# Three of eight convolution blocks as VectorE multiply-adds, shifted copies through DRAM, and second operands in PSUM, in a one-layer hybrid decoder block

## The chip, the cores and the metric

The kernel runs on one core of a Trainium2 chip. The metric is the device time of one launch in microseconds. TensorE is written PE in the rows, VectorE DVE, ScalarE ACT, GpSimd POOL, and SyncE, which issues the DMA transfers, SP. PEld is TensorE's weight load, which runs beside its matmuls.

## The reference, cut to what is computed

One layer, 256 tokens, 2048 channels, all in fp32. A norm is followed by one input projection that feeds two groups of heads; their outputs are joined and pass one output projection; then come a squared-ReLU MLP of 8192 channels and a gated embedding.

```python
h = rms_norm(x, norm_mix_pre)
z = h @ w_in                                   # 2048 -> 3360 (RWKV) + 2048 (conv)
z_rwkv = z[:, :3360] + (shift(z[:, :3360]) - z[:, :3360]) * mu
y_rwkv = rwkv7_time_mix(z_rwkv, ...)           # 16 heads of 64, recurrent over tokens
y_conv = conformer_conv(z[:, 3360:])
mixed = concat(y_rwkv, y_conv) @ w_out
x = x + rms_norm(mixed, norm_mix_post)
f = square(relu(rms_norm(x, norm_mlp_pre) @ w_up)) @ w_down
x = x + rms_norm(f, norm_mlp_post)
x = x + sigmoid(x @ w_ple_gate) * rms_norm(p @ w_ple, norm_ple)

def conformer_conv(z):                         # 1024 channels
    u = z_lin * sigmoid(z_gate)
    c = causal_depthwise_conv(u, dw_w, width=31) + dw_b
    c = (c - mean(c)) * rsqrt(var(c) + eps) * ln_gain + ln_bias   # over the channels
    return silu(c)
```

## The kernel before

Activations lie transposed: 128 channels on the partitions, 256 tokens along a row. Every product with a large weight is made in three parts (high part by high part, high by low, low by high): a 1 MB weight unit `W` comes by DMA, ScalarE casts quarters of it to `wh`, GpSimd (at times VectorE) subtracts to get `wl`, and TensorE runs 16 steps of three matmuls into a PSUM bank `acc` (lines 434 to 436; 439 to 442 where two parts share an instruction). There are two `W` buffers, seven `wh`/`wl` quarters and, in the first half of the layer, two `acc` banks; the tags `wk` and `inv` have two banks each, `seq` and `psy` one.

The order of instructions is fixed when the kernel is built. Each piece of work is a generator that yields operations; a planner (class `Plan`) keeps a clock for each engine with estimated costs (`tt`, `stt`, `ts`, `act`, `copy`, `pe`, `dma_in`), takes the operation that can start first, and among those that can start within 40 ns on that engine the one with the lowest priority number. The instructions then run on each engine, and on SP's DMA queue, in exactly this order and wait for their inputs. The helpers give many operations one line: 246 is any VectorE `tt`, 252 any `stt`, 248 any GpSimd `tt`, 276, 277 and 285 ScalarE, 231 any load.

The first half has 43 input tiles in an order written out by hand (`ORDER`: "p" a pair of heads with its tiles k, r, v; "c" a convolution block with its tiles linear and gate): p0, c0, c1, p1, p2, c2, c3, p3, c4, c5, c6, p4, c7, p5, p6, p7. Then come 32 half tiles of the output projection, first the convolution half, then the RWKV half. A tile's result is evicted by a generator: `zshift` for the pairs' tiles (VectorE multiplies by the norm into `zp`, ScalarE scales it into `zt`, VectorE combines both), `ev_lin` and `ev_gate` for the convolution. Each pair then runs `decay`, `keys`, `chunk_mats`, `values`, `bonus`, `inverse`, `recur` and `group_norm`; `recur` is serial over the pairs.

A convolution block of 128 channels (`taps`, priority 4) puts four shifted copies of `u`, each for 32 channels at a time, into the staging tile `cvst`: 16 matmuls with slices of the identity (line 1044) into `wk`, and two ScalarE copies. Then eight rounds of four matmuls with 32 columns each (line 1056) take four taps a round into an `inv` bank, with weights `cw` that come by DMA. An fp32 matmul stands twice in the rows. When all eight blocks are done, `layer_norm` (priority 1) runs over them on VectorE, GpSimd and ScalarE. The second half of the layer (up, down, gate) isn't touched by the diff.

## Time and profile before

| what | us |
|---|---|
| median of 3 runs (range) | 1400.93 (1400.87 to 1402.88) |
| the profiled execution's own time | 1402.03 |
| its span, first to last instruction | 1400.2 |
| TensorE busy, share of the span | 1351.5, 97% |
| GpSimd busy | 1174.2, 84% |
| ScalarE busy | 799.4, 57% |
| VectorE busy | 736.4, 53% |

The profiled execution is one run with the profiler on; its rows are from the slowest, here the only, core. Busy time is the union of an engine's instructions; matmuls overlap one another, so that a row's mean duration is longer than the distance between two starts. A wait is put down to the engine that released it last.

### The profile page before, as it was taken

The numbers are of one execution on the slowest core, as the hardware profiler recorded it, in microseconds if no ns is written. First come the engines' busy times: TensorE is split into PE (matmuls) and PEld (weight loads), VectorE is DVE, ScalarE is ACT, GpSimd is POOL, SyncE is SP. The second block draws the span as 40 slices with busy tenths as digits, with TensorE's granted clock in tenths as the row PEclk, the third lists the DMA queues.
The fourth block names the chain that finished last, engine by engine and source line by source line (L and its number), as shares of the span: only waits on it lengthen the run. The fifth ranks groups of instructions, "written<-read, shape, count | busy, mean of one in ns | idle before, by whom it ended". The sixth has DMA issues, their size and how long they took to land.

```text
span 1400.2 us, 27458 instructions
## 1 busy us (share of the span) xinstructions
PE 1351.5 (97%) x10476; PEld 1182.8 (84%) x10476; DVE 736.4 (53%) x1305; ACT 799.4 (57%) x1667; POOL 1174.2 (84%) x1002
## 2 busy tenths in 40 slices
PE   8999999999789999999999999999999999999898
PEld 7868878788778998788888888888888888889688
DVE  7256837235886545687003663236632266433694
ACT  6835665556657656855445554455554455555853
POOL 7765756576777769789999999999999999999787
PEclk9999999999899999999999999999999999999999
DMA  7442333433222465345555554555554555555353
GB/s 243 159 140 95 115 130 113 137 110 137 91 99 95 153 248 182 128 160 194 211 182 191 194 185 181 183 189 194 187 181 182 187 194 189 181 181 190 124 198 120
DMA packets 40354, 229.40 MB, mean 164 GB/s; under 512 B 6304, under 2 KB 9632, under 8 KB 14624
## 3 DMA queue, kind: packets, MB, share of 16 engines
q1 hardware_dynamic: 40224, 227.66, 46.0%
q8 instruction: 82, 1.34, 0.4%
q14 instruction: 48, 0.39, 0.1%
HBM read 225.55 MB, written 2.10 MB: 163 GB/s over the span
## 4 chain that ended last, share of the span: by engine, by line
PE 86%; DVE 8%; ACT 2%; issue 1%; DMA 1%; POOL 1%; SPq 0%; DVEq 0%; ACTq 0%; POOLq 0%
PE acc L441 34%; PE acc L442 17%; PE acc L434 8%; PE acc L435 7%; PE acc L436 7%; PE acc L440 3%; PE inv L1056 2%; PE acc L439 1%; PE wk L1044 1%; DVE hl L252 1%; DVE acc L246 1%; DVE acc L252 1%; PE psy L930 1%; PE seq L938 1%; PE wk L749 1%
## 5 line engine op out<-in xcount | busy, mean ns | idle before, releaser
L248 POOL TENSOR_TENSOR wl<-W,wh 128x512 fp32r<-128x512 f32 x548 | 734.4, 1353 | 119.2 <-ACT wh L285 99.3
L285 ACT CAST wh<-W 128x512 fp32r<-128x512 f32 x568 | 346.3, 618 | 220.3 <-PE acc L440 69.0
L441 PE MATMUL acc<-hl,wh 128*128 128x512 f32 x1016 | 369.8, 403 | 11.3 <-DVE hl L252 5.7
L441 PE MATMUL acc<-fhl,wh 128*128 128x512 f32 x806 | 288.2, 395 | 0.0
L442 PE MATMUL acc<-hl,wl 128*128 128x256 f32 x1016 | 286.5, 282 | 0.0
L434 PE MATMUL acc<-hl,wh 128*128 128x256 f32 (+1 forms) x928 | 282.1, 304 | 1.0 <-DVE zp L246 0.9
L436 PE MATMUL acc<-hl,wl 128*128 128x256 f32 (+1 forms) x928 | 265.2, 286 | 6.3 <-POOL wl L248 6.0
L435 PE MATMUL acc<-hl,wh 128*128 128x256 f32 (+1 forms) x928 | 265.7, 286 | 3.2 <-DVE hl L252 2.0
L248 POOL TENSOR_TENSOR wl<-Wb,wh 128x512 fp32r<-128x512 f32 x173 | 237.0, 1380 | 18.4 <-ACT wh L285 11.2
L441 PEld LDWEIGHTS acc<-hl,wh 128*128 128x128 f32 x1016 | 192.1, 189 | 60.2 <-DVE hl L252 8.4
L442 PE MATMUL acc<-fhl,wl 128*128 128x256 f32 x806 | 227.2, 282 | 0.0
L442 PEld LDWEIGHTS acc<-hl,wl 128*128 128x128 f32 x1016 | 193.2, 190 | 3.7
L434 PEld LDWEIGHTS acc<-hl,wh 128*128 128x128 f32 (+1 forms) x928 | 179.2, 193 | 15.6 <-issue 10.1
L246 DVE TENSOR_TENSOR gt<-acc,tb 128x256 f32<-128x256 f32 x124 | 52.4, 423 | 263.7 <-ACT tb L276 263.1
L436 PEld LDWEIGHTS acc<-hl,wl 128*128 128x128 f32 (+1 forms) x928 | 179.1, 193 | 7.3 <-POOL wl L248 6.6
L435 PEld LDWEIGHTS acc<-hl,wh 128*128 128x128 f32 (+1 forms) x928 | 179.5, 193 | 5.4 <-DVE hl L252 3.7
L441 PEld LDWEIGHTS acc<-fhl,wh 128*128 128x128 f32 x806 | 151.5, 188 | 33.4
L285 ACT CAST wh<-Wb 128x512 fp32r<-128x512 f32 x174 | 107.6, 621 | 89.4 <-PE acc L440 35.5
L442 PEld LDWEIGHTS acc<-fhl,wl 128*128 128x128 f32 x806 | 151.3, 188 | 2.7
L246 DVE TENSOR_TENSOR f<-f 128x256 f32<-128x256 f32 x63 | 85.9, 1366 | 1.9
L246 DVE TENSOR_TENSOR fhl<-f,fhl 128x256 fp32r<-128x256 f32 x62 | 58.5, 946 | 26.0 <-ACT fhl L276 26.0
L248 POOL TENSOR_TENSOR wlb<-W,whb 128x512 fp32r<-128x512 f32 x50 | 69.2, 1384 | 1.9 <-ACT whb L285 1.6
(319 smaller groups left out, 2004.2 us busy)
## 6 DMA issues: line engine op xcount, KB each, us to landing
W<-in_w_up_dram SPq DMA_DIRECT2D x43, 1024.0 KB, 4.8
W<-in_w_down_dram SPq DMA_DIRECT2D x42, 1024.0 KB, 4.8
W<-in_w_in_dram SPq DMA_DIRECT2D x38, 1024.0 KB, 4.9
Wb<-in_w_down_dram SPq DMA_DIRECT2D x22, 1024.0 KB, 4.8
Wb<-in_w_up_dram SPq DMA_DIRECT2D x21, 1024.0 KB, 4.8
W<-in_w_out_dram SPq DMA_DIRECT2D x14, 1024.0 KB, 4.8
W<-in_w_gate_dram SPq DMA_DIRECT2D x11, 1024.0 KB, 5.0
Wb<-in_w_gate_dram SPq DMA_DIRECT2D x5, 1024.0 KB, 4.8
```

The source lines that it names most:

```text
L246: alts.append((e, dve, lambda: nc.vector.tensor_tensor(out=out, in0=a, in1=b, op=op), None, pen))
L248: alts.append((e, 220 + 2.27 * n, lambda: nc.gpsimd.tensor_tensor(out=out, in0=a, in1=b, op=op), None, pen))
L252: return Op([("DVE", 210 + 1.042 * n + (0 if self.from_psum(R) or n < 128 else PORT), lambda: self.nc.vector.scalar_tensor_tensor(out=out, ...
L285: alts.append((e, 150 + 0.835 * n, lambda: self.nc.scalar.copy(out, a), None, 0))
L434: return [nc.tensor.matmul(o, h, xk[:, 0, :], start=(i == 0), stop=False), nc.tensor.matmul(o, h, xk[:, 1, :], start=False, stop=False), n ...
L435: nc.tensor.matmul(o, h, xk[:, 1, :], start=False, stop=False),
L436: nc.tensor.matmul(o, l, xk[:, 0, :], start=False, stop=(i == n - 1))]
L439: return [nc.tensor.matmul(a[:cols, T:], l, xk[:, 0, :], start=False, stop=False), nc.tensor.matmul(a[:cols, :], h, both, start=False, sto ...
L440: nc.tensor.matmul(a[:cols, :], h, both, start=False, stop=True)]
L441: return [nc.tensor.matmul(a[:cols, :], h, both, start=(i == 0), stop=False), nc.tensor.matmul(a[:cols, T:], l, xk[:, 0, :], start=False, ...
L442: nc.tensor.matmul(a[:cols, T:], l, xk[:, 0, :], start=False, stop=False)]
L1056: nc.tensor.matmul(ps.t[32 * g:32 * g + 32, :T], cw.t[:, g, m, :], cv.t[:, g, 4 * m:4 * m + T], start=(m == 0), stop=(m == 7)) for g in ra ...
```

## The change

It does four things. The shifted copies of the convolution no longer come from TensorE: `u` is stored to a DRAM tile `ur` and loaded four times, shifted, into `cvst`, all issued from SP's queue (`dma_move`). Blocks 2, 4 and 6 (`DCONV`) take another way altogether: 31 multiply-adds of VectorE with one weight column each (`dw`, new columns of `vecs`), from a padded `u` (`ux`) into an `inv` bank. Several second operands and results that lay in SBUF now lie in the other half of a PSUM bank that is at hand (`zt` and the gate's sigmoid in `acc`, `n4` in its `wk` bank, `ud` in the `inv` bank, the group norm reads `psy` without a copy, its gain product goes to a `wk` bank), so those banks are given back later. The gate product is always VectorE's. The planner's cost for DMA issues changes with it.

```diff
-NV = _o + 3
+VOFF["dw"] = _o + 3
+NV = _o + 3 + 8 * WIDTH
+DCONV = [2, 4, 6]
...
         if eng == "DMA":
-            self.clock["SP"] = st + 60
-            self.dma = max(self.dma, st + 700) + c
-            en = self.dma + 1900
+            self.clock["SP"] = st + (func or 330)
+            if func:
+                en = max(self.dma, st + 700) + c + 3300
+            else:
+                self.dma = max(self.dma, st + 700) + c
+                en = self.dma + 1900
...
+    def dma_move(self, dst, src, nbytes, R, W, rel=()):
+        return Op([("DMA", nbytes / 150.0, lambda: self.nc.sync.dma_start(dst, src), 600, 0)], R, W, rel)
...
+    dr = pa.enter_context(tc.tile_pool(name="dr", bufs=2, space=bass.MemoryType.DRAM))
+    reg(dr, "ur", 2, [P, 3 + T])
...
-    def scaled(acc, o, W, cols=P):
+    def scaled(acc, o, W, cols=P, keep=False):
-        yield pl.tt(["DVE"], o, acc.t[:cols, :T], r.t[:cols], ALU.mult, T, [acc, r], [W], [acc])
+        yield pl.tt(["DVE"], o, acc.t[:cols, :T], r.t[:cols], ALU.mult, T, [acc, r], [W], [] if keep else [acc])
     def zshift(acc, o, W, mu, j=0, cols=P):
-        yield from scaled(acc, zp.t[:cols, 1:], zp, cols)
+        yield from scaled(acc, zp.t[:cols, 1:], zp, cols, True)
-        d = yield Take("zt", 1)
-        yield pl.act(d.t[:cols], zp.t[:cols, 1:], AF.Identity, T, [zp, "omu"], [d], scale=om)
+        d = acc.t[:cols, T:]
+        yield pl.act(d, zp.t[:cols, 1:], AF.Identity, T, [zp, "omu"], [(acc, "d")], scale=om)
-        yield pl.stt(o, a, mu, b, ALU.mult, ALU.add, T, [d, zp, (zp, 0), "vt"], [W], [d, zp])
+        yield pl.stt(o, a, mu, b, ALU.mult, ALU.add, T, [(acc, "d"), zp, (zp, 0), "vt"], [W], [acc, zp])
...
-        n4 = yield Take("n4")
+        n4, kn = psn.t[:, 4:8], (psn, "n")
...
-        ud = yield Take("ud")
+        pe = yield Take("inv")
+        ud, kd = pe.t[:, T:T + 32].rearrange("p (c j) -> p c j", c=NC), (pe, "t")
...
-        ysb = yield Take("ysb")
-        yield pl.copy(["ACT"], ysb.t.rearrange("p a t -> p (a t)"), psy.t[:, :T], T, [(psy, False), (psy, True)], [ysb], [psy])
-        pl.spawn(group_norm(j, ysb), 1.1)
+        pl.spawn(group_norm(j, psy), 1.1)
...
-        pgn = yield Take("psy")
+        pgn = yield Take("wk", 2)
-        yield pl.stt(bv.t, pgn.t[:, :T], vec("gn_gain", j), bv.t, ALU.mult, ALU.add, T, [pgn, bv], [bv], [pgn])
+        yield pl.stt(pgn.t[:, T:], pgn.t[:, :T], vec("gn_gain", j), bv.t, ALU.mult, ALU.add, T, [pgn, bv], [(pgn, 1)], [bv, pgn])
-        yield pl.stt(y.t[:, j, :], bv.t, vec("gn_bias", j), gs.t, ALU.add, ALU.mult, T, [bv, gs], [(y, j)], [bv, gs])
+        yield pl.stt(y.t[:, j, :], pgn.t[:, T:], vec("gn_bias", j), gs.t, ALU.add, ALU.mult, T, [(pgn, 1), gs], [(y, j)], [pgn, gs])
...
     def ev_gate(j):
-            yield from scaled(acc, gt.t, gt)
-            yield pl.act(gt.t, gt.t, AF.Sigmoid, T, [gt], [gt])
+            yield from scaled(acc, gt.t, gt, keep=True)
+            yield pl.act(acc.t[:, T:], gt.t, AF.Sigmoid, T, [gt], [(acc, "d")], [gt])
-            yield pl.tt(PD, lin, lin, gt.t, ALU.mult, T, [gt, u], [u], [gt])
-            pl.spawn(taps(j), TAP + 0.01 * j)
+            yield pl.tt(["DVE"], lin, lin, acc.t[:, T:], ALU.mult, T, [(acc, "d"), u], [u], [acc])
+            pl.spawn((taps_dve if j in DCONV else taps)(j), TAP + 0.01 * j)
...
     def taps(j):
-        for b in range(2):
-            pr = yield Take("wk")
-            for g in (2 * b, 2 * b + 1):
-                o = (g % 2) * T
-                yield pl.pe(600, lambda: [
-                    nc.tensor.matmul(pr.t[32 * i:32 * i + 32, o:o + T], ident[:, 32 * g:32 * g + 32],
-                                     u.t[:, i:i + T], start=True, stop=True) for i in range(4)],
-                            [u, (u, 0), "fc"], [pr], [u] if g == 3 else [])
-            yield pl.copy(["ACT"], cv.t[:, 2 * b:2 * b + 2, 28:], pr.t.rearrange("p (g t) -> p g t", g=2), 2 * T,
-                          [pr], [(cv, b)], [pr])
+        ur = yield Take("ur")
+        yield pl.dma_move(ur.t, u.t, P * (3 + T) * 4, [u, (u, 0)], [ur], [u])
+        for i in range(4):
+            yield pl.dma_move(cv.t[32 * i:32 * i + 32, :, 28:], ur.t[:, i:i + T].rearrange("(g c) t -> c g t", g=4),
+                              P * T * 4, [ur], [(cv, i)] + [cv] * (i == 0), [ur] if i == 3 else [])
...
+    def taps_dve(j):
+        u = cvs[j]["u"]
+        b = yield Take("inv")
+        ac = b.t[:, :T]
+        for n in range(WIDTH):
+            w = vt[:, VOFF["dw"] + j * WIDTH + n:VOFF["dw"] + j * WIDTH + n + 1]
+            x_ = u.t[:, n:n + T]
+            if n == 0:
+                yield pl.ts(["DVE"], ac, x_, w, None, ALU.mult, None, T, [u, (u, 0), "vt"], [b])
+            else:
+                yield pl.stt(ac, x_, w, ac, ALU.mult, ALU.add, T, [u, b], [b], [u] if n == WIDTH - 1 else [])
+        yield from conv_out(j, b, ac)
```

`conv_out` is the end of `taps` as before (bias, and the sum for the layer norm). Blocks in `DCONV` load no `cw`.

## Rows read from the trace of the kernel before

**Rows 1.** The page's first part: busy time, share of the span and instructions of each engine.

```profile
PE 1351.5 (97%) x10476; PEld 1182.8 (84%) x10476; DVE 736.4 (53%) x1305; ACT 799.4 (57%) x1667; POOL 1174.2 (84%) x1002
```

**Rows 2.** Busy time by stage: stretch and its length in us, then for each engine busy us and instructions, the granted TensorE clock, the busy share of the DMA engines, GB/s.

```profile
0.00:70.00 70.00, 64.59 (x446) 56.52 (x447) 34.73 (x54) 51.21 (x110) 52.16 (x67) 1.00 0.61 201
70.00:170.00 100.00, 92.22 (x1127) 78.72 (x1126) 71.36 (x151) 50.76 (x113) 66.79 (x76) 0.97 0.35 118
170.00:343.00 173.00, 170.32 (x2155) 143.59 (x2155) 83.06 (x213) 100.55 (x209) 107.70 (x112) 1.00 0.39 129
343.00:432.00 89.00, 72.72 (x745) 67.27 (x743) 75.22 (x168) 55.49 (x127) 69.31 (x83) 0.94 0.28 99
432.00:510.00 78.00, 77.90 (x927) 73.50 (x927) 39.57 (x110) 51.44 (x129) 55.71 (x52) 0.96 0.35 124
...
575.00:1400.00 825.00, 814.48 (x4668) 708.19 (x4666) 393.92 (x537) 448.77 (x892) 771.42 (x575) 1.00 0.51 181
```

**Rows 3.** The chain that ended last: its share by engine (from the page) and by line, then some of its pieces in order of time (start and length in us).

```profile
PE 86%; DVE 8%; ACT 2%; issue 1%; DMA 1%; POOL 1%; SPq 0%; DVEq 0%; ACTq 0%; POOLq 0%
by line: PE acc L441 34.0%; PE acc L442 17.3%; PE acc L434 7.5%; PE acc L435 6.7%; PE acc L436 6.6%; PE acc L440 2.6%; PE inv L1056 2.2%; issue 1.3%; PE acc L439 1.3%; PE wk L1044 1.2%; DVE hl L252 0.7%; DVE acc L246 0.6%; DVE acc L252 0.6%
180.45 1.00 PE wk L1044 x16
249.82 1.00 PE wk L1044 x16
292.69 1.00 PE wk L1044 x16
296.86 3.59 PE inv L1056 x64
428.34 1.51 DVE hl L246
```

**Rows 4.** Groups of TensorE's instructions from 0 to 650 us: line, engine, operation, output and inputs, shape, count, then busy us and mean ns of one, then the idle time before them. Below them two matmuls of an input tile in order of time.

```profile
L1056 PE MATMUL inv<-cvst,cw 128*32 128x256 f32 x512 | 31.8, 383 | 0.0
L1044 PE MATMUL wk<-u,fc 128*32 128x256 f32 x256 | 19.1, 395 | 1.9 <-DVE bv L246 1.9
...
328.98 0.28 PE L435 MATMUL acc<-hl,wh 128*128 128x256 f32 x1
329.10 0.28 PE L436 MATMUL acc<-hl,wl 128*128 128x256 f32 x1
```

**Rows 5.** TensorE's longest wait from 70 to 343 us (first row) and from 343 to 432 us (last row): what waited, for what, us in total, times, longest.

```profile
PE wk L783 <- DVE rbst L246: 2.1, 2, 1.8
...
PE acc L436 <- POOL wl L248: 6.0, 3, 4.1
```

**Rows 6.** Groups of VectorE's instructions from 0 to 650 us, shapes kept apart; columns as in rows 4.

```profile
L252 DVE SCALAR_TENSOR_TENSOR acc<-mac,vt,pb 128x256 f32<-128x256 f32 x14 | 6.6, 485 | 0.4
L252 DVE SCALAR_TENSOR_TENSOR vd<-zp,vt,zt 128x256 f32<-128x256 f32 x8 | 7.1, 886 | 0.8 <-ACT zt L277 0.7
L252 DVE SCALAR_TENSOR_TENSOR zk<-zp,vt,zt 128x256 f32<-128x256 f32 x8 | 6.1, 758 | 6.2 <-ACT zt L277 5.5 <-POOL csq L248 0.7
L252 DVE SCALAR_TENSOR_TENSOR zr<-zp,vt,zt 128x256 f32<-128x256 f32 x8 | 5.9, 734 | 1.7 <-ACT zt L277 1.7
L252 DVE SCALAR_TENSOR_TENSOR y<-bv,vt,gs 128x256 f32<-128x256 f32 x8 | 7.2, 901 | 0.2
L283 DVE CAST udh<-ud 128x32 fp32r<-128x32 f32 x8 | 5.4, 670 | 0.1
L246 DVE TENSOR_TENSOR udl<-ud,udh 128x32 fp32r<-128x32 f32 x8 | 2.0, 246 | 0.2
L246 DVE TENSOR_TENSOR cen<-ysb,s 128x256 f32<-128x256 f32 x8 | 4.7, 582 | 0.4
L246 DVE TENSOR_TENSOR u<-u,gt 128x256 f32<-128x256 f32 x3 | 2.3, 777 | 1.8 <-ACT gt L277 1.8
```

**Rows 7.** Groups of ScalarE's and GpSimd's instructions from 0 to 570 us; columns as in rows 4.

```profile
L277 ACT ACTIVATE zt<-zp,omu 128x256 f32<-128x256 f32 x26 | 12.9, 505 | 17.7 <-DVE zp L246 17.5
L285 ACT COPY cvst<-wk 128x512 f32<-128x512 f32 x16 | 9.4, 587 | 16.6 <-PE wk L1044 16.4
L285 ACT COPY ysb<-psy 128x256 f32<-128x256 f32 x8 | 3.0, 371 | 5.9 <-PE psy L930 5.8
L248 POOL TENSOR_TENSOR wl<-W,wh 128x512 fp32r<-128x512 f32 x216 | 283.9, 1327 | 89.0 <-ACT wh L285 76.0 <-issue 6.2 <-PE wk L769 1.3
L248 POOL TENSOR_TENSOR u<-u,gt 128x256 f32<-128x256 f32 x5 | 3.3, 651 | 2.0 <-PE psy L930 1.1 <-ACT gt L277 0.9
```

**Rows 8.** VectorE in order of time near 370 us: start and length in us, line, operation, output and inputs, count, and in brackets the idle time before it.

```profile
367.80 0.40 DVE L246 TENSOR_TENSOR zp<-acc,rstd 128x256 f32<-128x256 f32 x1
376.19 2.97 DVE L246 TENSOR_TENSOR y<-y,sqt 128x256 f32<-128x256 f32 x2
379.91 0.47 DVE L252 SCALAR_TENSOR_TENSOR vd<-zp,vt,zt 128x256 f32<-128x256 f32 x1
```

**Rows 9.** DMA issues of the whole span: output and input, count, KB each, median us from issue to landing.

```profile
out_dram<-os SPq DMA_DIRECT2D x16, 128.0 KB, 1.8
gup<-in_w_gup_dram SPq DMA_DIRECT2D x8, 128.0 KB, 5.1
```

**Rows 10.** What the DMA queue waited for from 0 to 560 us: us in total, times, longest.

```profile
SPq L231 <- POOL wl L248: 350.6, 47, 19.1
```

More of the change, by code (lines that the diff above doesn't have):

```diff
@@ L836, in inverse @@
                     m8[:, None, :, None].to_broadcast(sh), ALU.mult, T, Uk + ["fc"], [um])
[L837 to L839 removed]
+        pe = yield Take("inv")
+        ud, kd = pe.t[:, T:T + 32].rearrange("p (c j) -> p c j", c=NC), (pe, "t")
+        yield pl.vec(555, lambda: nc.vector.tensor_reduce(out=ud, in_=um.t.rearrange("p c q j -> p c j q"),
+                                                          axis=mybir.AxisListType.X, op=ALU.add), [um], [kd], [um])
         udh = yield Take("udh")
         udl = yield Take("udl")
[L842 to L843 removed]
+        yield pl.copy(["DVE"], udh.t, ud, 32, [kd], [udh])
+        yield pl.tt(["DVE"], udl.t, ud, udh.t.bitcast(F32), ALU.subtract, 32, [kd, udh], [udl])
         es = []
@@ L1012, in f @@
         def f(acc):
-            u = yield Take("u")
-            cw = yield Take("cw")
-            yield pl.dma_in(cw.t, w_cv[j], P * 1024 * 4, [cw])
-            yield pl.memset(u.t[:, 0:3], 0.0, [(u, 0)], 3)
-            yield from scaled(acc, u.t[:, 3:], u)
-            cvs[j]["u"], cvs[j]["cw"] = u, cw
+            if j in DCONV:
+                u = yield Take("ux")
+                yield pl.memset(u.t[:, 0:WIDTH - 1], 0.0, [(u, 0)], 30)
+            else:
+                u = yield Take("u")
+                cvs[j]["cw"] = cw = yield Take("cw")
+                yield pl.dma_in(cw.t, w_cv[j], P * 1024 * 4, [cw])
+                yield pl.memset(u.t[:, 0:3], 0.0, [(u, 0)], 3)
+            yield from scaled(acc, u.t[:, u.t.shape[1] - T:], u)
+            cvs[j]["u"] = u
         return f
@@ L1057, in taps, with conv_out @@
                                  start=(m == 0), stop=(m == 7)) for g in range(4)],
-                        [cw, (cv, 0), (cv, 1)], [ps], [cw, cv] if m == 7 else [])
-        yield pl.act(a, ps.t[:, :T], AF.Identity, T, [ps], [ka], [ps], bias=vec("dw_b", j))
+                        [cw] + [(cv, i) for i in range(4)], [ps], [cw, cv] if m == 7 else [])
+        yield from conv_out(j, ps, ps.t[:, :T])
+    def taps_dve(j):
[7 more added lines that the diff above has]
+                yield pl.ts(["DVE"], ac, x_, w, None, ALU.mult, None, T, [u, (u, 0), "vt"], [b])
+            else:
+                yield pl.stt(ac, x_, w, ac, ALU.mult, ALU.add, T, [u, b], [b], [u] if n == WIDTH - 1 else [])
+        yield from conv_out(j, b, ac)
+    def conv_out(j, ps, src):
+        y = S["y"]
+        a = y.t[:, NP + j, :]
+        ka = (y, NP + j, "c")
+        yield pl.act(a, src, AF.Identity, T, [ps], [ka], [ps], bias=vec("dw_b", j))
         if cdone[0] == 0:
```

43 lines of the change are left out of this document (19 added, 24 removed).

## The prediction

> **What bounds the kernel now.** The page comes first. TensorE is busy 97% of the span, GpSimd 84%, VectorE 53%, ScalarE 57% [rows 1]. An average says nothing of stages, so the second view is the table by stage [rows 2]. From 575 us on, TensorE is busy 814 of 825 us; the diff touches nothing there, and I carry it over unchanged. The layer's first half, in which all edits lie, ends near 575 us, and its stages differ. From 170 to 343 us TensorE is busy 170.32 of 173 us at a granted clock of 1.00, and VectorE only 83.06. From 343 to 432 us it is the other way round: TensorE has 16 us idle and a clock of 0.94, VectorE is busy 75.22 of 89. From 432 to 510 us TensorE is full again (77.90 of 78). So convolution work on TensorE up to 343 us sits in a stretch that TensorE paces, and a microsecond taken from it should move all that follows.
>
> The third view, the chain that ended last, is the test of that. TensorE's matmuls carry 86% of it, and the two lines of the convolution stand in it by themselves: L1056 (the eight accumulated taps) with 2.2% and L1044 (the shifted copies by slices of the identity) with 1.2% of 1400.2 us, that is 30.8 and 16.8 us [rows 3]. The group rows give nearly the same as busy time, 31.8 and 19.1 us [rows 4]. The work really is on the path. One block's 64 matmul instructions of L1056 take 3.59 us in the chain's row, and blocks 2, 4 and 6 start their L1044 work at 180, 250 and 293 us [rows 3].
>
> The fourth view is TensorE's waits. Between 70 and 343 us it is idle for 10.5 us in all [rows 2], and the largest group of waits is 2.1 us [rows 5]; no single engine is late there. Between 343 and 432 us the largest is 6.0 us, for `wl` of GpSimd: there the layer norm of the convolution and the pairs 5 to 7 share VectorE and GpSimd.
>
> **The change part by part.**
>
> *Identity matmuls out.* L1044 goes for all eight blocks: 16.8 us of the chain. The eight L1056 rounds go for three of eight blocks: 3/8 of 30.8 is 11.6 us. Together 28.4 us off the path (by busy time 19.1 + 11.9 = 31.0). Its bounds are 0, if none of it were on the path (third rival), and -31. I take -28.4, since the chain carries it.
>
> *Multiply-adds on VectorE in.* `taps_dve` is 31 instructions of 128x256 for each of blocks 2, 4, 6: 93 in all, one input in SBUF, the running sum in PSUM. The nearest row is `acc<-mac,vt,pb`, of the same kind and placement: 485 ns [rows 6]. 93 x 0.485 = 45.1 us of VectorE. They all fall in what is now 170 to 343 us. VectorE has 90 us idle there; but the stretch shrinks by the saving in it (six of the eight blocks' L1044, 12.6 us, and 11.6 us of L1056) to about 149 us, and VectorE's load rises to 83 + 45 = 128, less some 8 us of the next edit: 120 of 149, 81%. That is no longer roomy. The row for 343 to 432 us, with VectorE at 85%, shows TensorE idle for 18%; the row for 70 to 170 us, with VectorE at 71%, for 8% [rows 2]. So the price lies between nothing (the multiply-adds have priority 4, behind all pair work, and each blocks VectorE for half a microsecond only) and 18% of 149 us, 27 us. What speaks for the low end: a pair that is late here makes TensorE run another input tile, since at 1.5% idle it always had one. I take +5.
>
> *Second operands in PSUM.* The 24 token-shift results (`zk`, `zr`, `vd`) take 758, 734 and 886 ns on average with two SBUF inputs [rows 6]; at 485 ns they save 7.4 us. `y` at 901 saves 3.3, the cast `udh` at 670 against 246 for its neighbour `udl` 3.4, `cen` at 582 0.8; the gate product, now always on VectorE, costs eight times at most 485 ns, 1.6 us more than its three instances of 777 did. Net 13 us of VectorE. ScalarE loses sixteen copies of 587 ns and eight of 371 (12 us), GpSimd five gate products of 651 ns (3 us) [rows 7]. Most of it lies beside TensorE and is worth nothing by itself; what falls into 343 to 432 us, where VectorE paces (nine token shifts and two or three group norms of it, about 5 us), can count. Bounds: 0 and -6. I take -3.
>
> This is where the Trainium skill bears on the case. SBUF — State Buffer, "Who interferes with whom", says that a VectorE instruction with two SBUF inputs and a GpSimd instruction that reads SBUF exclude each other for their whole length, and one with a single SBUF input doesn't. The rows agree: 485 ns with one input in PSUM against means of 734 to 901 with none. By that rule GpSimd's split (1327 ns) would quicken too, which I count as nothing.
>
> *Banks held longer.* The other side of it: `acc` (two banks) is now given back after the last instruction of a token shift, not after the first, and for the gate after the product. That adds a ScalarE step of 505 ns [rows 7], a VectorE step of 485 and whatever VectorE has queued between. Where VectorE has room that is 1 to 2 us, inside the 5.7 us that TensorE spends on the other bank (16 steps x 3 matmuls, starting 0.12 us apart [rows 4]): free. Around 368 us it isn't: `zp` of one tile is written at 367.80 and its `vd` only at 379.91 [rows 8], 12 us, more than a tile. Bounds 0 and +6 for such cases; I take +2. `taps_dve` also keeps one of the two `inv` banks for 15 us or more; the pairs' inverses, which take `inv` in a strict row, get by with the other.
>
> *DRAM copies.* For blocks 0, 1, 3, 5, 7 the sync queue issues a store of `u` (130 KB) that waits for the gate product, and four loads of 128 KB that wait for the store; behind them stand the weight loads. The nearest rows: a 128 KB store lands in 1.8 us, a 128 KB load amid weight traffic in 5.1 [rows 9]. A block's copies so take about 7 us against some 4.5 us for L1044 and its two ScalarE copies, and the queue is held for the store's 1.8 us plus issues. Cover: this queue waited 350.6 us in 47 weight loads for GpSimd to free a buffer [rows 10], 7.5 us for each, so a hold of 2 to 3 us delays no load. The convolution itself isn't urgent: its layer norm ends near 379 us [rows 8], and the split of its result for the output projection begins at 428 [rows 3], when the last input tile has let go of the one `hl` buffer. I take +1, bounds 0 and +35 (five blocks, 7 us, without cover). DMA: Bandwidth & Descriptors, "Anatomy of one DMA", in the Trainium skill puts a fixed cost of about 2 us on each transfer; an estimate from that page is 4 us for store and loads in series, less than by the rows, and the sum stays as it is.
>
> *Constants.* `vecs` grows by 248 columns, 124 KB, ahead of the first `x` load. The first 70 us move 201 GB/s [rows 2], so 0.6 us late at the start, of which I count +0.5. Three `cw` loads (512 KB) go, off the path.
>
> Sum: -28.4 + 5 - 3 + 2 + 1 + 0.5 = -22.9. The profiled execution took 1402.03 us, 1.1 above the median of 1400.93; the change goes on the median: **1378 us**. Bounds of the terms put this case between 1364 (-31 of TensorE's work, -6 for the PSUM operands, nothing for the rest) and 1392, with the multiply-adds at half the 27 us and the DRAM copies at 7.
>
> **The rivals.**
>
> *VectorE becomes the pace of 170 to 343 us.* For it: 81% load, and the two rows in which TensorE idles while VectorE is that busy. Against it: in those rows the VectorE work is urgent (layer norm, recurrence), here it is filler. Price 18 to 27 us instead of 5: the time is 1391 to 1400. I give it 0.16: 0.10 of that faster, 0.05 within 0.2% (2.8 us, about what a measurement of this kernel can tell from no change) and 0.01 slower.
>
> *The sync queue starves the split (slower).* The place is the store's wait for `u` and the first load's wait for the store, with weight loads queued behind. If the gate product comes later on the chip than in the written-out order, the queue stands still for that long too. It decides once a hold passes the 7.5 us of slack per load plus the split tiles in stock (seven quarters, 28 steps of 0.36 us, 10 us). At 35 us for five blocks the saving of 28.4 is gone and the sum is 1401 - 23 + 34 = 1412. Against it: the slack row. 0.13.
>
> *The saving stays off the path.* If the pairs' serial recurrence, not TensorE, sets when 432 us comes, a shorter first stretch only lengthens the idle time in 343 to 432 us: 1400 or so. For it: that stretch already waits for VectorE and GpSimd. Against it: pairs 4 to 7 enter by input tiles in TensorE's order, which come earlier by the saving. 0.05.
>
> **How the numbers follow.** The forecast has 0.66, the rivals 0.16, 0.13 and 0.05. Faster by more than 0.2%: 0.66 + 0.10 = 0.76. Within 0.2%: 0.05 of the first rival and 0.04 of the third, 0.09. Slower: 0.13, and 0.01 each of these two, 0.15. The range reaches from 1364, the low bound, into the first rival up to 1397 and leaves out the slower one.
>
> **What would show it.** No rows of `wk<-u,fc`, and 160 instead of 256 matmuls, 320 as the rows count them, on the line that reads `cvst`; 90 rows of the multiply-add near 485 ns and three of the first product; token shifts near 485 ns; TensorE still above 95% busy in the stretch before the layer norm, which starts some 22 us earlier; the stage from the first up-projection on as long as before (825 us). Wrong would be: TensorE waits behind `acc` or `inv` from VectorE of more than 10 us, waits of the split for a weight DMA, or a longer stretch between the last convolution and the first output-projection tile.

## The result, and the profile after

The changed kernel takes 1350.24 us (median; 1347.14 to 1352.90) against 1401.91 us (1400.87 to 1404.23) of the kernel before on the same chip: a ratio of 0.963 (0.960 to 0.966), 51.7 us less. The forecast was 22.9 us less. The direction is right, the gain is more than twice as large, and the time lies below 1364 us, the low end of the forecast's range. Its profiled execution took 1351.71 us, with a span of 1349.9.

The page's first part, of the kernel after:

```profile
PE 1315.4 (97%) x10028; PEld 1168.8 (87%) x10028; DVE 759.4 (56%) x1404; ACT 782.7 (58%) x1639; POOL 1167.0 (86%) x997
```

TensorE has 36.1 us less to do than in [rows 1], while the span is 50.3 us shorter. The work that was taken out doesn't explain the whole gain. To see where the rest came from, both traces are cut at the same events: the first eviction of a convolution's linear tile, the layer norm's first subtraction, the token shift of the last input tile, the first eviction of the RWKV half of the output projection, and the first gather of the up-projection. Busy time by stage, columns as in [rows 2]; the kernel before first:

```profile
0.00:63.30 63.30, 57.89 (x390) 49.82 (x391) 33.13 (x48) 44.59 (x100) 47.46 (x62) 1.00 0.62 206
63.30:345.30 282.00, 271.55 (x3354) 231.26 (x3354) 157.34 (x371) 159.08 (x335) 180.65 (x195) 0.99 0.37 125
345.30:431.70 86.40, 70.42 (x727) 65.02 (x725) 73.61 (x164) 54.06 (x123) 67.55 (x79) 0.94 0.29 102
431.70:511.70 80.00, 78.66 (x931) 74.06 (x932) 40.97 (x112) 52.13 (x131) 57.71 (x53) 0.96 0.36 127
511.70:583.20 71.50, 65.76 (x453) 60.18 (x452) 43.12 (x93) 48.27 (x110) 56.27 (x47) 0.95 0.51 190
583.20:1400.20 817.00, 807.28 (x4630) 702.42 (x4628) 388.20 (x523) 441.30 (x873) 764.55 (x570) 1.00 0.51 182
```

The same table of the kernel after:

```profile
0.00:68.60 68.60, 60.50 (x390) 51.93 (x391) 33.13 (x50) 47.08 (x105) 46.14 (x61) 0.93 0.58 194
68.60:322.00 253.40, 249.74 (x3004) 228.16 (x3003) 195.97 (x487) 152.03 (x320) 187.95 (x199) 1.00 0.46 153
322.00:386.40 64.40, 58.03 (x653) 53.69 (x651) 56.22 (x149) 44.74 (x110) 52.78 (x66) 0.97 0.28 99
386.40:459.90 73.50, 72.42 (x868) 67.99 (x869) 41.59 (x108) 49.17 (x124) 56.33 (x53) 0.95 0.35 128
459.90:536.00 76.10, 69.61 (x492) 63.83 (x491) 42.78 (x93) 49.93 (x112) 58.96 (x50) 0.98 0.51 191
536.00:1349.90 813.90, 805.15 (x4630) 703.19 (x4628) 389.75 (x523) 439.74 (x873) 764.83 (x570) 1.00 0.51 183
```

By length the stages changed by +5.3, -28.6, -22.0, -6.5, +4.6 and -3.1 us. The second stage, where the convolution runs, is 28.6 us shorter, near the 28.4 us that were forecast to come off TensorE. That match is partly luck: the convolution's work there fell by 30.7 us (below), 98 matmul instructions of other work with 8.9 us moved in, and 6.8 us of idle time went. The third, from the layer norm to the last input tile, gives 22 us, where the forecast had about 3.

The second to fourth stages together went from 448.4 to 391.3 us, -57.1. Four things make that up. TensorE's convolution work falls from 31.8 + 19.1 = 50.9 us [rows 4] to 20.2, -30.7. TensorE's idle time (length less busy) falls from 10.45 + 15.98 + 1.34 = 27.8 us to 3.66 + 6.37 + 1.08 = 11.1, -16.7. The time at the lower clock falls: if the clock is either 1.2 or 2.4 GHz, a mean granted clock of 0.94 over 86.4 us means 2 x 0.06 x 86.4 = 10.4 us at 1.2 GHz, and the three stages sum up to about 22 us before and 11 after. That is worth half of the difference, 5 to 6 us (an estimate from rounded clocks). The last 4 us are work that now lies behind the first RWKV half tile: the fifth stage has 39 more matmul instructions and 3.9 us more TensorE work, and is 4.6 us longer.

Groups of the kernel after that answer to [rows 4, 6, 7], columns as there:

```profile
L1063 PE MATMUL inv<-cvst,cw 128*32 128x256 f32 x320 | 20.2, 383 | 0.0
L261 DVE SCALAR_TENSOR_TENSOR inv<-ux,vt,inv 128x256 f32<-128x256 f32 x90 | 43.5, 483 | 1.6
L261 DVE SCALAR_TENSOR_TENSOR zk<-zp,vt,acc 128x256 f32<-128x256 f32 x8 | 3.8, 474 | 0.6 <-ACT acc L286 0.4
L261 DVE SCALAR_TENSOR_TENSOR y<-wk,vt,gs 128x256 f32<-128x256 f32 x8 | 3.8, 478 | 0.2
L255 DVE TENSOR_TENSOR cen<-psy,s 128x256 f32<-128x256 f32 x8 | 3.4, 422 | 0.2
L257 POOL TENSOR_TENSOR wl<-W,wh 128x512 fp32r<-128x512 f32 x216 | 283.0, 1323 | 86.2 <-ACT wh L294 75.4 <-PE acc L445 3.6 <-PE acc L444 3.3
```

The larger operations came out at the size that the forecast gave them: the multiply-add 483 ns (485 forecast), token shifts 474 (485), the group norm's `y` 478 (485, from 901). Some small ones came out cheaper: `cen` 422 (485), the cast `udh` 182 (246), the gate product 411 (at most 485), under 2 us of VectorE in all. What came out otherwise in the main is the order and the waiting.

The order shows on VectorE. Two instructions in order of time, of the kernel before: the layer norm's first subtraction (`y<-y,wk`) and the first mask of pair 5's chunk matrices (`U<-wk,fc`):

```profile
345.27 0.42 DVE L246 TENSOR_TENSOR y<-y,wk 128x256 f32<-128x256 f32 x1 [0.36 <-PE wk L1070]
...
389.69 0.41 DVE L246 TENSOR_TENSOR U<-wk,fc 64x256 f32<-64x256 f32 x1 [1.29 <-PE wk L749]
```

The same two, of the kernel after:

```profile
319.09 0.42 DVE L255 TENSOR_TENSOR U<-wk,fc 64x256 f32<-64x256 f32 x1 [1.56 <-PE wk L760]
...
321.96 0.40 DVE L255 TENSOR_TENSOR y<-y,wk 128x256 f32<-128x256 f32 x1
```

Before, pair 5 comes 44 us behind the layer norm; after, 3 us ahead of it. The layer norm has priority 1 in the planner, and it starts as soon as the eight blocks are done. Pair 5 is the first of three pairs whose recurrences follow one another. That gives a theory: the unforecast gain comes from the turned order, since the serial chain of pairs 5 to 7 is what the third and fourth stages wait for. The rivals are that it comes from VectorE's shorter instructions there (the PSUM operands), or that each part simply is worth more than was put down for it.

### The profile page after: what moved, and what is told of

Same layout as the page of the kernel before. It is cut to its first block, busy times and chain, and to the rows that moved or that the text cites. A ratio compares the mean times of both kernels' runs of the same rounds, so it can differ in the third digit from the quotient of the medians.

```text
span 1349.9 us, 26673 instructions
## 1 busy us (share of the span) xinstructions
PE 1315.4 (97%) x10028; PEld 1168.8 (87%) x10028; DVE 759.4 (56%) x1404; ACT 782.7 (58%) x1639; POOL 1167.0 (86%) x997
## 4 chain that ended last, share of the span: by engine, by line
PE 67%; DVE 3%; ACT 1%; issue 0%; ACTq 0%
PE acc L450 35%; PE acc L451 18%; PE acc L443 3%; PE acc L444 3%; PE acc L445 3%; PE acc L449 3%; PE acc L448 1%; DVE acc L255 1%; DVE acc L261 1%; DVE hl L261 0%; ACT xT L294 0%; DVE hl L255 0%; ACT hl L286 0%; PE psy L941 0%; ACT hl L285 0%
## 5 line engine op out<-in xcount | busy, mean ns | idle before, releaser
L294 ACT CAST wh<-W 128x512 fp32r<-128x512 f32 x565 | 345.3, 618 | 218.3 <-PE acc L450 86.3
L450 PE MATMUL acc<-hl,wh 128*128 128x512 f32 x1045 | 375.6, 400 | 10.6 <-DVE hl L261 6.5
L450 PE MATMUL acc<-fhl,wh 128*128 128x512 f32 x837 | 297.2, 395 | 0.0
L451 PE MATMUL acc<-hl,wl 128*128 128x256 f32 x1045 | 293.8, 281 | 0.0
L257 POOL TENSOR_TENSOR wl<-Wb,wh 128x512 fp32r<-128x512 f32 x175 | 241.1, 1395 | 13.6 <-ACT wh L294 10.9
L450 PEld LDWEIGHTS acc<-hl,wh 128*128 128x128 f32 x1045 | 197.2, 189 | 59.3 <-DVE hl L261 9.6
L451 PE MATMUL acc<-fhl,wl 128*128 128x256 f32 x837 | 235.5, 281 | 0.0
L451 PEld LDWEIGHTS acc<-hl,wl 128*128 128x128 f32 x1045 | 198.5, 190 | 3.1
L450 PEld LDWEIGHTS acc<-fhl,wh 128*128 128x128 f32 x837 | 157.3, 188 | 34.7
L451 PEld LDWEIGHTS acc<-fhl,wl 128*128 128x128 f32 x837 | 157.0, 188 | 2.9
```

What stands on the lines that cost most here:

```text
L257: alts.append((e, 220 + 2.27 * n, lambda: nc.gpsimd.tensor_tensor(out=out, in0=a, in1=b, op=op), None, pen))
L294: alts.append((e, 150 + 0.835 * n, lambda: self.nc.scalar.copy(out, a), None, 0))
L450: return [nc.tensor.matmul(a[:cols, :], h, both, start=(i == 0), stop=False), nc.tensor.matmul(a[:cols, T:], l, xk[:, 0, :], start=False, ...
L451: nc.tensor.matmul(a[:cols, T:], l, xk[:, 0, :], start=False, stop=False)]
```

## The experiments

The runs were made on several chips; the kernel before had medians of 1401.2 to 1402.2 us beside them, so that medians compare to about 1 us across chips. Ratios are against the kernel before on the same chip, with a 95% interval.

### Each part alone

Kernel `e1_psum`, the second operands in PSUM alone: of the diff mainly `scaled(..., keep)`, `zshift`, `n4`, `ud`, the group norm and the gate product, with `DCONV` empty.

```diff
+DCONV = []
...
-        d = yield Take("zt", 1)
+        d = acc.t[:cols, T:]
...
-            yield pl.tt(PD, lin, lin, gt.t, ALU.mult, T, [gt, u], [u], [gt])
+            yield pl.tt(["DVE"], lin, lin, acc.t[:, T:], ALU.mult, T, [(acc, "d"), u], [u], [acc])
```

> The kernel before with the second operands in PSUM alone (token shift, gate, n4, ud, group norm); matmul convolution with the identity copies as before. Sum of parts, as in the prediction: -3 + 2, so 1400 (1395 to 1406). Rival, the PSUM operands shorten the stretch from the layer norm to the last input tile: 20 to 28 us less, 1373 to 1382, with that stretch near 62 us instead of 83. Rival, the order of pair 5 and the layer norm: not touched here, 1400.

Measured: 1393.49 us, ratio 0.994 (0.992 to 0.996), -7.7. Busy time of its third stage:

```profile
343.50:423.50 80.00, 70.89 (x755) 66.31 (x753) 67.09 (x161) 52.38 (x119) 62.14 (x76) 0.91 0.30 102
```

VectorE does 67.1 us instead of 73.6, and the stage is 6.4 us shorter. That fits the forecast's reading that VectorE's work sets the length there, and it would put the term at its bound of -6 instead of -3. But the second stage is 6.2 us shorter too (275.8) and the first 4.4 longer (67.7), so that the stage nearly equals the whole gain by chance. Pair 5's mask still comes 37 us behind the layer norm.

Kernel `e2_dram`, the DRAM copies alone, for all eight blocks: only `dma_move`, `ur`, the planner's cost and this part of `taps`:

```diff
-                    nc.tensor.matmul(pr.t[32 * i:32 * i + 32, o:o + T], ident[:, 32 * g:32 * g + 32],
...
+        yield pl.dma_move(ur.t, u.t, P * (3 + T) * 4, [u, (u, 0)], [ur], [u])
```

> The kernel before with the shifted copies through DRAM for all eight blocks, the rest as before. Sum of parts: -16.8 + 1.6, about 1386. Rival, PSUM operands shorten the later stretch: the same 1386. Rival, order (the copies let block 7 end after pair 5's tiles, so that pair 5 no longer stands behind the layer norm): some 20 us more, 1362 to 1368, with the first mask of pair 5 (U) ahead of the layer norm's first subtraction.

Measured: 1394.37 us, ratio 0.995 (0.993 to 0.996), -7. It takes all 16.8 us of identity matmuls out and keeps less than half of that. Its third and fourth stages:

```profile
335.30:410.20 74.90, 61.97 (x610) 56.60 (x608) 65.36 (x145) 43.05 (x99) 59.13 (x72) 0.93 0.30 103
410.20:503.40 93.20, 84.36 (x965) 78.08 (x966) 42.21 (x114) 52.96 (x134) 61.73 (x58) 0.89 0.31 111
```

The fourth stage takes 93.2 us instead of 80.0, with 8.8 us of idle TensorE and a clock of 0.89. This is the third rival's mechanism, one stage later than the rival had it: work taken off ahead of the layer norm came back as waiting behind it.

Kernel `e3_dve`, the VectorE blocks alone: `taps_dve` for blocks 2, 4 and 6, the other five with identity matmuls as before. `n4` and `ud` lie in PSUM here too, for room.

```diff
+DCONV = [2, 4, 6]
...
-            pl.spawn(taps(j), TAP + 0.01 * j)
+            pl.spawn((taps_dve if j in DCONV else taps)(j), TAP + 0.01 * j)
```

> The kernel before with blocks 2, 4, 6 as multiply-adds of VectorE; identity copies for the other five, second operands in SBUF except n4 and ud (kept in PSUM for room), one tag for both kinds of u. Sum of parts: L1044 of three blocks -6.3, L1056 -11.6, +5, so about 1388. Rival, VectorE paces: 1400 or more, with the stretch up to the layer norm not shorter. Rival, order: 1388 if pair 5 still stands behind the layer norm, 1368 if not.

Measured: 1374.83 us, ratio 0.981 (0.979 to 0.982), -26.4. It takes three eighths of both lines off TensorE, 18 us, and brings more than that.

### Two parts together

Kernels `e5_psum_dve` (without the DRAM copies), `e6_psum_dram` (without the VectorE blocks), `e7_dram_dve` (without the PSUM operands). Each is the changed kernel's diff less that part, but `e7_dram_dve` keeps `n4` and `ud` in PSUM, as `e3_dve` does. The planner's new cost for DMA issues stands in the kernels with DRAM copies only:

> Changed kernel without the DRAM copies: identity copies for the five blocks that stay on TensorE, at the old planner costs. If the parts add up as measured alone (PSUM -8, VectorE blocks -26): 1367. If the missing 10 us of the whole belong to these two together (VectorE's multiply-adds and the pairs' operands compete for one engine): 1355 to 1358.

> Changed kernel without VectorE blocks: all eight by matmul, copies through DRAM, second operands in PSUM. Additive: -8 - 7, 1386. If the DRAM copies alone lost their gain in the wait for the last pair (11 us between the last input tile and the RWKV half of the output projection) and the PSUM operands shorten that chain: 1374 to 1378, with that stretch back near 80 us.

> Changed kernel with the token shift, the gate and the group norm in SBUF as before. Additive: -7 - 26, 1368. By the prediction's sum for these two (-28.4 of TensorE's work, +5, +1): 1378. If the missing 10 us belong to these two: 1358.

Measured: 1368.58 us (0.977, 0.975 to 0.978), 1369.34 (0.977, 0.975 to 0.979) and 1353.26 (0.966, 0.964 to 0.968). All eight combinations, medians in us:

| | without DRAM copies | with DRAM copies | the copies bring |
|---|---|---|---|
| neither | 1401.9 | 1394.4 | -7.5 |
| PSUM operands | 1393.5 | 1369.3 | -24 |
| VectorE blocks | 1374.8 | 1353.3 | -21.5 |
| both | 1368.6 | 1350.2 | -18 |

The parts don't add. The DRAM copies are worth 7 us alone and 18 to 24 in company. The PSUM operands are worth 8 alone, 25 beside the copies and 3 beside the copies and the VectorE blocks. A constant price for each part, the last rival, falls with this table, and the rival of the PSUM operands with `e7_dram_dve`: without them in the token shift, the gate and the group norm, it is 3 us from the changed kernel. The two kernels with copies and VectorE blocks (`e7_dram_dve` and the changed one) are the only ones of these in which pair 5's mask comes ahead of the layer norm (316.1 and 319.1 us for `e7_dram_dve`), and they are the fastest.

### The order by itself

Kernel `e9_ln_after_pair5`: the kernel before, in which the layer norm waits until pair 5's operand `BKT` is there.

```diff
-        yield Wait(lambda: cdone[0] == NP)
+        yield Wait(lambda: cdone[0] == NP and "BKT" in prs[5])
```

> The kernel before; the layer norm additionally waits until pair 5's masks and transposed keys are there. Theory: VectorE paces the stretch from the layer norm to the last input tile, and its length is VectorE's work in it; if some 10 us of pair 5's work go ahead of the layer norm as in the changed kernel, the last token shift comes 8 to 16 us earlier and the total is 1387 to 1394. Rival: the order of the two doesn't matter, the sum of VectorE's work up to the last input tile does: 1399 to 1404.

Measured: 1392.83 us, ratio 0.993 (0.991 to 0.994), -9.2 with no work added or taken out. Its fourth stage:

```profile
425.50:504.50 79.00, 76.79 (x940) 72.14 (x941) 43.17 (x122) 52.93 (x133) 61.86 (x58) 0.98 0.38 135
```

It is 79.0 us long, hardly shorter than the 80.0 of before. Most of the gain came ahead of it: the last token shift is at 425.5 instead of 431.7.

Kernel `e10_pair5_late`: the changed kernel, in which the chunk matrices of pairs 5 to 7 wait, in the written-out order, until the layer norm has its mean and variance (its last passes over the eight blocks are only queued then).

```diff
-        yield Wait(lambda: all(n in pr for n in ("kkr", "kp", "bk", "Ep", "Em", "zr")))
+        yield Wait(lambda: all(n in pr for n in ("kkr", "kp", "bk", "Ep", "Em", "zr")) and (j < 5 or "ln" in S))
...
+        S["ln"] = True
```

> The changed kernel; pairs 5 to 7 make their masks only after the layer norm has been written out, as the kernel before happened to do for pair 5. Theory of order: 8 to 16 us lost, 1358 to 1366, the stretch from the layer norm to the last token shift some 75 us instead of 64. Rival: 1348 to 1353.

Measured: 1373.59 us, ratio 0.980 (0.978 to 0.981). That is 23.4 us more than the changed kernel, with all of the change in it, and lies 4.4 us from the forecast. Its third and fourth stages, and the fourth cut in three:

```profile
320.50:377.30 56.80, 49.71 (x408) 46.83 (x406) 46.84 (x100) 40.31 (x88) 46.93 (x59) 0.94 0.27 96
377.30:480.00 102.70, 90.02 (x1116) 81.55 (x1117) 57.08 (x168) 55.48 (x144) 62.29 (x61) 0.83 0.28 98
...
377.30:393.00 15.70, 11.81 (x202) 10.29 (x202) 15.03 (x38) 8.38 (x22) 14.90 (x15) 0.89 0.32 112
393.00:424.00 31.00, 22.21 (x264) 17.41 (x265) 15.98 (x51) 13.60 (x37) 7.67 (x14) 0.50 0.04 17
424.00:480.00 56.00, 56.00 (x652) 53.85 (x652) 26.07 (x80) 33.50 (x85) 39.73 (x34) 1.00 0.40 139
```

The input tiles are through early, the third stage is even 7.6 us shorter, and then there is little but the recurrence: from 393 to 424 us TensorE runs its short matmuls with 8.8 us of gaps, at the lower clock throughout (0.50, 1.2 GHz), and the DMA engines carry 4%. The fourth stage takes 102.7 us instead of 73.5. So what this order costs has two parts, the gaps themselves and the clock that is low with them. It isn't the order of the kernel before, though: all three pairs are held back, and the fourth stage is far longer than the 80.0 us there.

Kernel `e13_dram_ln_after`: `e2_dram` with the wait of `e9_ln_after_pair5`.

> DRAM copies alone (as in the second run), with the layer norm made to wait for pair 5's masks. That part alone gave 1394 and lost 11 us between the last input tile and the RWKV half of the output projection, with 13.7 us of slow clock there. If pair 5 behind the layer norm is what loses it: 1376 to 1383, that stretch near 80 us instead of 93. If the copies themselves hold up the later part: 1391 to 1397.

Measured: 1372.56 us, ratio 0.978 (0.976 to 0.980), 21.8 less than `e2_dram`. Its fourth stage:

```profile
405.10:478.40 73.30, 72.16 (x898) 68.20 (x898) 42.48 (x118) 49.34 (x124) 57.34 (x54) 0.95 0.38 137
```

The 93.2 us have become 73.3. With the order held, the DRAM copies bring 20.3 us (1392.8 to 1372.6) instead of 7.

Kernel `e14_psum_dve_ln_after`: `e5_psum_dve` with the same wait.

> PSUM operands and VectorE blocks without DRAM copies (1368.6), with the layer norm made to wait for pair 5's masks. If what the DRAM copies add to these two (18 us) is mainly that block 7 ends later and the layer norm so comes behind pair 5: 1356 to 1361. If it is only their 10.5 us of matmuls on five blocks: 1367 to 1371.

Measured: 1368.12 us, ratio 0.976 (0.973 to 0.979), no gain over the 1368.58 of `e5_psum_dve`. There the layer norm was 21 us ahead of pair 5 too, but the fourth stage already had only 71.4 us:

```profile
404.80:476.40 71.60, 69.50 (x879) 65.99 (x880) 38.39 (x104) 45.00 (x116) 56.06 (x50) 0.98 0.45 155
```

So the same wait was worth 9.2, 21.8 and 0.5 us in three kernels. Pair 5's place against the layer norm doesn't say which kernel has a long fourth stage. `e6_psum_dram` has pair 5 17 us behind the layer norm, and its fourth stage is short all the same:

```profile
406.40:477.70 71.30, 70.44 (x869) 66.81 (x870) 38.91 (x107) 47.62 (x120) 53.32 (x50) 0.98 0.36 129
```

Another mark does sort the kernels: the first mask of the last of the three pairs. Of the kernel before, of `e10_pair5_late` and of the changed kernel, in this order:

```profile
456.96 0.42 DVE L246 TENSOR_TENSOR U<-wk,fc 64x256 f32<-64x256 f32 x1
...
426.41 0.42 DVE L255 TENSOR_TENSOR U<-wk,fc 64x256 f32<-64x256 f32 x1 [0.86 <-PE wk L760]
...
401.39 0.42 DVE L255 TENSOR_TENSOR U<-wk,fc 64x256 f32<-64x256 f32 x1 [0.24 <-PE wk L760]
```

Distances in us (a minus: ahead of it):

| kernel | pair 5's mask behind the layer norm | last pair's mask behind the last token shift | fourth stage |
|---|---|---|---|
| before | 44 | 25 | 80.0 |
| `e9_ln_after_pair5` | -13 | 22 | 79.0 |
| `e2_dram` | 16 | 44 | 93.2 |
| `e13_dram_ln_after` | -13 | 16 | 73.3 |
| `e5_psum_dve` | 21 | 13 | 71.4 |
| `e14_psum_dve_ln_after` | -8 | 4 | 71.6 |
| `e6_psum_dram` | 17 | 14 | 71.3 |
| `e10_pair5_late` | 39 | 49 | 102.7 |
| changed | -3 | 15 | 73.5 |

In all 17 traces a fourth stage of 71 to 74 us has the last pair's mask 4 to 18 us behind the last token shift, and one of 77 to 103 us has it 22 to 49 us behind. This is read off the traces; no run moved the last pair alone.

Kernels `e4_ln_late` and `e8_order`, the kernel before with one priority number changed: the layer norm's (`LNP`) from 1.0 to 2.5, and, in the second kernel, the taps' (`TAP`) from 4.0 to 2.15.

```diff
-TAP, LNP, AFP = 4.0, 1.0, 3.5
+TAP, LNP, AFP = 4.0, 2.5, 3.5
...
+TAP, LNP, AFP = 2.15, 1.0, 3.5
```

> The kernel before with one number changed: the layer norm of the convolution gets priority 2.5, behind all pair work, instead of 1.0. Theory of order: pair 5 no longer waits for the layer norm, the stretch from it to the last input tile shrinks by 15 to 20 us, total 1381 to 1388. Rival, PSUM operands and less work on VectorE make the difference: no change, 1398 to 1403, or slower if the output projection then waits for the layer norm.

> The kernel before with one number changed: the convolution's priority 2.15 instead of 4, so that its work stands in the order among the pairs' and not behind it. No work is added or removed. If TensorE's 28 us of idle time between the first convolution tile and the RWKV half of the output projection have fixed causes: 1398 to 1404, idle 25 to 31. If they are a matter of the order that the planner happens to find: the time moves by 5 us or more either way, and the idle time with it.

Measured: 1403.76 us (1.001, 1.000 to 1.002) and 1400.01 (0.999, 0.998 to 1.000). A lower priority of the layer norm alone brings nothing. Pair 5's mask does come 17 us earlier (372.8), but the last input tile's shift comes at 436.4 instead of 431.7, and the third stage runs at a clock of 0.87:

```profile
344.60:436.40 91.80, 80.30 (x903) 73.78 (x902) 69.33 (x173) 59.38 (x137) 72.50 (x88) 0.87 0.28 96
```

The layer norm's operations were spread between the pairs' instead of moved behind them. And `e8_order` is one reshuffle of the list that leaves pair 5 behind the layer norm (385.3 against 341.2 us): it is worth some 2 us, not 20.

### The prices in dispute

Kernel `e11_idle_taps`: the kernel before with 93 multiply-adds of VectorE added to blocks 2, 4 and 6, of the same size and at the same place; nobody reads their result, and the convolution is still made on TensorE.

```diff
+            if j in IDLE:
+                pl.spawn(idle(j), TAP + 0.005 + 0.01 * j)
...
+        for n in range(WIDTH):
+            x_ = u.t[:, n % 4:n % 4 + T]
...
+                yield pl.stt(ac, x_, w, ac, ALU.mult, ALU.add, T, [u, b], [b], [u, b] if n == WIDTH - 1 else [])
```

> The kernel before with 93 multiply-adds of VectorE added whose sum nobody reads: for blocks 2, 4, 6, after the gate product, into an inv bank, beside the unchanged matmul convolution. It prices VectorE's part by itself. Prediction: +5, 1406. Rival of the prediction, VectorE becomes the pace: +18 to +27, 1420 to 1428. Theory now: they fit into VectorE's idle time, 0 to +2, 1401 to 1404.

Measured: 1404.7 us, ratio 1.002 (1.001 to 1.003), +2.7. Their group:

```profile
L253 DVE SCALAR_TENSOR_TENSOR inv<-u,vt,inv 128x256 f32<-128x256 f32 x90 | 43.5, 484 | 1.7
```

45 us of VectorE work cost less than 3.

Kernel `e12_wa_bank`: the changed kernel with the scaled operand of the first token shift (`wa`) in SBUF again, so that its `acc` bank comes free after the first instruction, and with only 93 weight columns.

```diff
+        early = mu == "mu_wa"
+        yield from scaled(acc, zp.t[:cols, 1:], zp, cols, not early)
...
-NV = _o + 3 + 8 * WIDTH
+NV = _o + 3 + 3 * WIDTH
```

> The changed kernel, but the token shift of the first tile (decay and rate) keeps its scaled copy in SBUF and gives its acc bank back after the first product; only three blocks' weight columns in the constants (31 KB less each of five). If the 2.9 us in which TensorE waits for that shift, and the slow clock behind it, are the price of the bank held longer: 3 to 5 us faster than the changed kernel, 1345 to 1348. If something else at the start costs it: 1349 to 1351.

Measured: 1349.05 us, ratio 0.962 (0.960 to 0.963), not clear of the changed kernel's 1350.24. TensorE's longest wait from 30 to 70 us, first of the changed kernel, then of this one:

```profile
PE acc L443 <- DVE wa L261: 2.9, 1, 2.9
```

```profile
PE acc L443 <- DVE zp L255: 0.9, 1, 0.9
```

The wait is gone and the first stage back at 63.9 us instead of 68.6, but the next stage takes 256.6 us instead of 253.4, and the end gains 1.2 us at most.

Kernel `e15_four_blocks`: the changed kernel with a fourth block on VectorE.

```diff
-DCONV = [2, 4, 6]
+DCONV = [1, 2, 4, 6]
```

> The changed kernel with a fourth block (1) as multiply-adds of VectorE; only these blocks' weight columns in the constants. One more block takes 3.8 us of matmuls and a 512 KB load away and adds 15 us to VectorE between 70 and 170 us, where it is busy 72%. If VectorE still has room: 1345 to 1348. If that stretch is then paced by it: 1352 to 1360.

Measured: 1348.3 us, ratio 0.961 (0.958 to 0.964), not clear of the changed kernel either. Its second stage:

```profile
66.10:315.90 249.80, 246.10 (x2940) 226.07 (x2939) 207.66 (x514) 151.77 (x323) 191.83 (x206) 1.00 0.43 148
```

VectorE is busy 83% of it and TensorE idle for 3.7 us: even a fourth block doesn't make VectorE the pace.

## Why the prediction was half right, step by step

*Convolution's matmuls out: right.* Forecast -28.4 us by the chain, -31.0 by busy time. Busy time fell by 30.7. The convolution's stage is 28.6 us shorter, a match that is partly luck, as said above. The layer norm starts 23.3 us earlier (322.0 against 345.3), where 22 was forecast.

*Multiply-adds in: mechanism right, size too high.* Forecast +5; alone +2.7 (`e11_idle_taps`). In the changed kernel's second stage VectorE is busy 196.0 of 253.4 us, 77%, and TensorE idle for 3.7, less than the 10.5 of before. The first rival, VectorE as the pace, falls. That fits the reason given for the low end: filler of half a microsecond a piece delays little, while in the third stage before, with urgent work and VectorE busy 85%, TensorE was idle for 16.0 of 86.4 us.

*Second operands in PSUM: too low.* Forecast -3 with a bound of -6; alone -7.7, with its third stage at -6.4, its second at -6.2 and its first at +4.4. The large durations were right, but I let only half of the stretch's share count, and what the part brings depends on the others, from 3 to 25 us.

By the Trainium skill, SBUF — State Buffer, "Who interferes with whom", a VectorE instruction with two SBUF inputs contends with a GpSimd instruction that reads SBUF, and one with at most one, outside the 2-port modes, doesn't. VectorE's side agrees: 474 to 483 ns with one input in PSUM, after means of 734 to 901 [rows 6]. GpSimd's split, which the forecast thought would quicken by this rule, took 1323 ns after 1327 [rows 7]: by this trace no gain.

*Banks held longer: +2, right as a kind, wrong as to place.* I looked for it near 368 us. It shows at the start: the wait of 2.9 us for `wa` above, in a stage that is 5.3 us longer (4.4 in `e1_psum`). `e12_wa_bank` takes that away, together with five blocks' weight columns, and gains 1.2 us at most, so the term is worth 0 to +2.

*DRAM copies: cover right, a block's copies longer than thought.* DMA issues, the queue's waits (0 to 520 us), and the split's wait for weights (75 to 312 us), of the kernel after, answering to [rows 9, 10]:

```profile
cvst<-ur SPq DMA_DIRECT2D x20, 128.0 KB, 5.7
ur<-u SPq DMA_DIRECT2D x5, 129.5 KB, 2.1
```

```profile
SPq L237 <- POOL wl L257: 307.9, 45, 18.9
...
SPq L240 <- DVE u L255: 10.7, 2, 5.9
SPq L240 <- DVE rh L292: 6.4, 1, 6.4
...
SPq L240 <- DVE Y L255: 4.6, 1, 4.6
...
SPq L240 <- DMA ur<-u: 1.1, 2, 0.9
```

```profile
ACT wh L294 <- DMA W<-in_w_in_dram: 2.2, 2, 1.6
```

The store landed in 2.1 us (1.8 forecast), a load in 5.7 (5.1). But the four loads are issued one after another: for block 7 the store is issued at 299.42 us and the last load at 303.3, which by an estimate from these numbers makes some 10 us for a block's copies, where 7 were forecast. The 2 us a transfer that the forecast named from the Trainium skill (DMA: Bandwidth & Descriptors, "Anatomy of one DMA") don't fit the loads; that section is headed for transfers that GpSimd issues, and these are issued by SyncE.

The queue stood 22.8 us in all ahead of the copies (line 240), 6.4 at the longest, and still waited 307.9 us for GpSimd to free a weight buffer. ScalarE's cast, the first step of the split, waited for weights twice, 2.2 us in all. So the loads had slack, and the second rival, the starved split, falls.

*The rest of the first half unchanged: this is the step that failed.* The forecast said of the stretch from 343 to 432 us that VectorE paces it and that "about 5 us can count", and otherwise carried it and the 78 us behind it over, merely shifted. Its reason was that the pairs enter by input tiles, which come earlier by the saving; what the order of the work makes of the stretch it put at nothing. But the stretch isn't a fixed length. From the layer norm to the first RWKV half tile it went from 166.4 to 137.9 us, -28.5, where -3 was forecast. The order alone, with no work added or taken out, takes 9.2 us off the kernel before (`e9_ln_after_pair5`) and 21.8 off the kernel with DRAM copies (`e13_dram_ln_after`), and puts 23.4 on the changed kernel (`e10_pair5_late`). So it is shown that the time behind the convolution depends on the order, which the forecast held fixed.

How much of the 28.8 us that the forecast lacks is due to pair 5's turn isn't shown; it depends on the kernel from which one looks. From the changed kernel it is 23.4, which is likely too much, since `e10_pair5_late` makes a longer fourth stage than the kernel before had (102.7 against 80.0); that it lands near the forecast is partly luck. From the kernel before it is 9.2: with the layer norm behind pair 5 on both sides, the change still brings 42.6 us (1392.8 to 1350.2). And by way of `e5_psum_dve` it is nothing that can be told from noise. That kernel is 33.3 us faster than the one before with pair 5 still behind the layer norm, turning the two there brings 0.5, and the DRAM copies then bring 18 with the order held.

The view that would have told it was at hand: the third and fourth stages had 17.3 us of idle TensorE and about 17 us at the lower clock, more than any other stage of the first half, and the forecast treated that as a given instead of asking what orders it. The third rival saw the same stretch, but only as a place where time could be lost; that the change might also alter the order and win time was in neither forecast nor rivals.

Why does the order turn? The layer norm starts when the last block is done, and from block 7's gate product to its output there are now more microseconds. The two instructions before:

```profile
331.43 0.65 POOL L248 TENSOR_TENSOR u<-u,gt 128x256 f32<-128x256 f32 x1 [0.23 <-ACT gt L277]
...
342.43 0.47 ACT L277 ACTIVATE y<-inv,vt 128x256 f32<-128x256 f32 x1 [0.34 <-PE inv L1056]
```

And after:

```profile
298.98 0.42 DVE L255 TENSOR_TENSOR u<-u,acc 128x256 f32<-128x256 f32 x1
...
317.49 0.47 ACT L286 ACTIVATE y<-inv,vt 128x256 f32<-128x256 f32 x1 [0.29 <-PE inv L1063]
```

It is 11.0 us before and 18.5 after, while the product comes 32 us earlier. The way through DRAM is part of the longer path (the store is issued at 299.42, the loads from 301.69 on, 5.7 us each). So pair 5 gets 7.5 us more of VectorE ahead of the layer norm. That this decided the order is argued from the two traces and was not tried by itself. It can't be the whole reason, since `e6_psum_dram` takes the same way through DRAM and leaves pair 5 behind.

*From the first up-projection on: nearly right.* 825 us were to stay; by the same events it is 817.0 before and 813.9 after. No run explains these 3.1 us.

Two things stay open. With the order held in both, the DRAM copies bring 18 us (1368.1 to 1350.2) beside the other two parts, while the identity matmuls of the five blocks are worth 5/8 of 16.8, 10.5 us; no run says where the other 7.5 come from. A rival that wasn't tried is the planner's new cost for DMA issues: it came in with the copies in every run, and it can alter the order by itself. And no run says what sets how late the last pair's mask comes.

## What to carry to other kernels

Where a program's order is laid down when it is built, don't carry over a stretch in which the busiest engine idles and its clock is low as a fixed length: ask which serial chain it waits for, when the last link of that chain starts, and what stands ahead of it. Test a change of such a kernel with the order held as well as free, since the parts here were worth 7 to 24 us, 19 to 41 and 3 to 25 according to what else was in. A share of busy time didn't tell the pace here: half-microsecond filler at a low priority loaded VectorE to 77 and 83% with 3.7 us of idle TensorE in 250, while 85% with urgent work stood beside 16 us in 86.
